# Gate-and-up product of an FFN: P3 of group 1 placed between P6 and P4 of group 0, in the other pair of banks

## The chip, the cores and the metric

The kernel runs on one core of one Trainium2 chip. The metric is the device time of one execution in microseconds, from three runs. The kernel's main engines are TensorE (PE in the rows; PEld is its loading of stationary operands), VectorE (DVE), ScalarE (ACT), GpSimd (POOL) and SyncE (SP), which issues most plain DMAs.

## What is computed

A two-layer encoder trunk on 512 tokens of width 1024. Layer 0 mixes tokens by gated linear attention and RWKV-7, layer 1 by multi-head latent attention; after each mixer stands a SwiGLU FFN with 2816 hidden columns. What the change touches is the first half of that FFN, twice:

```python
def swiglu_ffn(x, w_gate_up, w_down):
    gu = x @ w_gate_up
    gate, up = gu[..., :FFN_HIDDEN], gu[..., FFN_HIDDEN:]
    return (jax.nn.silu(gate) * up) @ w_down

x = layer_norm(DN_ALPHA * x + swiglu_ffn(x, ffn_w_gate_up[i], ffn_w_down[i]), ln_g[i, 1], ln_b[i, 1])
```

## The kernel before

Every large product is done with split operands: a float32 matrix is cast to a high part (`wh`, `xh`) on ScalarE, the remainder is the low part (`wl`, `xl`) by a subtraction on VectorE (`split`, L190 to L193), and a product is high by high, high by low and low by high.

The gate-and-up product (`ffn`, L1139) treats the hidden columns in six groups, 512 columns wide for the first four and 384 for the last two. A group's product of 512 tokens by 1024 by gate and up columns is done with seven products of half size, P1 to P7 (a Strassen-Winograd scheme): each is a sum of parts of x, held in `xh`, `xl`, `Sh` and `Sl`, times a sum of blocks of the weights. P2 is added up in the banks of P1, and P4 in the banks of P7 (`chained`, L1277).

One product (`product`, L1227) has two halves, k2 = 0 and 1. Each half takes a buffer pair for the high and the low part (`parts`, L1214: two `wh`/`wl` pairs, and for every third half, where `spare` is set, the pair called `third`), splits 1024 columns of weights into it and runs 12 matmuls: eight with the high part, then four with the low part. So a product is 24 matmuls.

The weights of a group lie in three float32 buffers, X, Y and Z. X and Z are loaded by SyncE; Y holds in turn the weights of P3, P7, P6 and P4, and X those of P1 and P5. Between them the buffer is changed in place: `more` (L1264) has GpSimd issue two DMAs (512 KB each) that add another block of weights to it. They wait for the two splits that read the old contents, and the next product that reads the buffer waits for them to land.

After its matmuls a product's results are taken from the banks (`step`, L1276 to L1309): copies on ScalarE after P1, P3 and P7; subtractions, additions and multiplications on VectorE after P5 and P6 (eight operations after P6, L1302 to L1305); after P4, for each of the two token tiles, a subtraction on VectorE (L1307), Silu on ScalarE (L1308) and a multiplication on VectorE (L1309). Then `turn(0)` and `turn(1)` (L1311) transpose the finished halves `w` and `v` of the group on TensorE, eight transposes each into two `ps_s` banks, and ScalarE copies them to the hidden tile (L1318). `turn(0)` needs what P6 leaves, `turn(1)` what P4 leaves.

The accumulators (`banks`, L1224) are a pair of the four banks tagged `g`, or the pair `t` and `o`, one bank each. P5 uses t and o, and so does P1, save in group 1.

The order is written out in `work` (L1333): products of neighbouring groups are interleaved. From group 2 on it is P1 of the new group, P4 and turn(0) of the old one, P3, turn(1), P2, the loads of the next group, P7, P5, P6. For group 1, whose P1 and P2 come before the loop, it is P4 of group 0, P3 of group 1, turn(0), turn(1), the loads of group 2, P7, P5, P6. Within an engine the instructions run in a fixed order that the program's builder made from this; it is not always the written one, as the rows below show (a split can stand ahead of copies that are written before it).

Of the kernel before, what the change touches and what calls it, by code (L numbers as in the profile page):

```python
# [1138 lines left out]
def ffn(g, i, hid, ep):  # L1139
# [11 lines left out]
    def E(name):  # L1151
        return ep.tile([P, S], F32, tag="e", name=name, bufs=10)
# [48 lines left out]
    def sums(*names):  # L1201
        for n in names:
            for u in range(2):
                f = whole(u)
                o = {"P3": "P2", "P5": "P1"}.get(n, n)
                if o != n:
                    nc.vector.tensor_tensor(f[o], in0=f["P6"], in1=f[o], op=ALU.subtract)
                out(u, n, f[o])
# [15 lines left out]
    def banks(chain):  # L1224
        return [g.pp.tile([P, S], F32, tag=t, name="ps_g", bufs=4 if t == "g" else 1) for t in ("to" if chain else "gg")]

    def product(name, n, source, acc, first=True, spare=True):  # L1227


        A_ = A[name]  # L1230
        for k2 in range(2):
            h, l = parts(n, spare)
            split(nc, h, l, source(k2))
            for b, w in enumerate((h, l)):
                for q in range(2):
                    k = 2 * k2 + q
                    for u in range(2):
                        for a in range(2 - b):
                            nc.tensor.matmul(acc[u][:, :n], lhsT=A_[a][:, k, P * u:P * u + P], rhs=w[:, q], start=first and k + a + b == 0,  # L1239
                                             stop=k + b == 4, skip_group_check=True)  # L1240

    def group(j):
        c, n = GROUPS[j]
        w = g.I[f"w_gu{i}{j}"]
        W, T, acc, e = {}, {}, {}, [Ctx(), Ctx()]

        def place(k):

            if k == "Z" and j == 1:
                T[k] = [hid.tile(0)[:, 2 * k2:2 * k2 + 2].rearrange("p a b -> p (a b)") for k2 in range(2)]  # L1250
            elif k == "Z":
                T[k] = [g.wp.tile([P, 1024], F32, tag="w", name="w", bufs=2)[:, :2 * n] for k2 in range(2)]
            else:
                t = tp.tile([P, 2048], F32, tag="raw", name="raw", bufs=4)
                T[k] = [t[:, 2 * n * k2:2 * n * k2 + 2 * n] for k2 in range(2)]

        def load(k):
            if k not in T:
                place(k)
            r, q = {"X": (0, 0), "Y": (1, 1), "Z": (1, 0)}[k]  # L1260
            for k2 in range(2):
                nc.sync.dma_start(T[k][k2], w[r, q, k2])

        def more(k, r, q):  # L1264
            for k2 in range(2):
                nc.gpsimd.dma_start(T[k][k2], w[r, q, k2], accum_op=ALU.add)  # L1266

        def row(name, u, i):

            return (hid.row(4 + 2 * i + u) if j == 1 else E(name))[:, :n]  # L1270

        def dve(o, a, op, b):
            nc.vector.tensor_tensor(o, in0=a, in1=b, op=op)
            return o

        def step(name, spare=True):  # L1276
            chained = {"P2": "P1", "P4": "P7"}.get(name)  # L1277
            acc[name] = p = acc[chained] if chained else banks(name == "P5" or name == "P1" and j != 1)
            k = {"P1": "X", "P5": "X", "P2": "Z"}.get(name, "Y")
            product(name, n, lambda k2: T[k][k2].rearrange("p (q n) -> p q n", q=2), p, chained is None, spare)  # L1280
            if name in ("P1", "P3", "P7", "P6"):
                more(k, *{"P1": (0, 1), "P3": (0, 1), "P7": (0, 0), "P6": (1, 0)}[name])
            add, sub = ALU.add, ALU.subtract
            for u in range(2):
                d, y = e[u], p[u][:, :n]
                if name == "P1":
                    d.s1 = row("s1", u, 0)
                    nc.scalar.copy(d.s1, y)
                elif name == "P2":
                    d.g = row("g", u, 1)  # L1290
                    nc.scalar.activation(d.g, y, AF.Silu)
                elif name == "P3":
                    d.w = E("w")[:, :n]
                    nc.scalar.copy(d.w, y)
                elif name == "P7":
                    d.v = E("v")[:, :n]
                    nc.scalar.copy(d.v, y)
                elif name == "P5":
                    dve(d.w, y, add, d.w)
                    dve(d.v, y, add, d.v)  # L1300
                elif name == "P6":
                    d.u = dve(E("u")[:, :n], y, sub, d.s1)  # L1302
                    dve(d.w, d.u, sub, d.w)
                    dve(d.w, d.w, ALU.mult, d.g)
                    dve(d.v, d.u, sub, d.v)  # L1305
                else:
                    dve(d.u, y, sub, d.u)  # L1307
                    nc.scalar.activation(d.u, d.u, AF.Silu)  # L1308
                    dve(d.v, d.v, ALU.mult, d.u)  # L1309

        def turn(half):  # L1311
            for u in range(2):
                y = (e[u].w, e[u].v)[half]
                t = 2 * half + u
                p = g.pp.tile([P, S], F32, tag="s", name="ps_s", bufs=2)[:, :n]
                for m in range(n // P):
                    nc.tensor.transpose(out=p[:, m * P:(m + 1) * P], in_=y[:, m * P:(m + 1) * P], identity=g.C("ident"))  # L1317
                nc.scalar.copy(hid.tile(j)[:, :, t * P:(t + 1) * P], p.rearrange("p (m t) -> p m t", t=P))  # L1318

        return Ctx.of(place=place, load=load, step=step, turn=turn)  # L1320

    gs = [group(j) for j in range(len(GROUPS))]
# [10 lines left out]
    def work():  # L1333

        gs[0].step("P2", False)
        sums("P3")
        gs[0].step("P3", False)
        gs[1].step("P2", False)
        sums("P7", "P5", "P6")
        last = len(gs) - 1  # L1340
        for j, x in enumerate(gs):
            more = j < 4
            if j:
                if j > 1:
                    x.step("P1", more)
                gs[j - 1].step("P4", more)
                if j > 1:
                    gs[j - 1].turn(0)
            if j:
                x.step("P3", more)  # L1350
                for h in range(0 if j == 1 else 1, 2):
                    gs[j - 1].turn(h)
            if j > 1:
                x.step("P2", more)
            if 0 < j < last:
                gs[j + 1].load("Z")
                gs[j + 1].load("X")
                gs[j + 1].load("Y")
            x.step("P7", more and j > 0)
            x.step("P5", more)  # L1360
            x.step("P6", more)
        gs[last].step("P4", False)
        return [lambda h=h: gs[last].turn(h) for h in range(2)]

    return Ctx.of(sink=sink, again=again, load=load, begin=begin, work=work)


# [455 lines left out]
```

## Time and profile before

| | us |
|---|---|
| runs (three) | 1384.99, 1387.27, 1394.15 |
| median | 1387.27 |
| profiled execution, its own time | 1391.69 |
| span of the profile, first to last instruction | 1389.6 |
| TensorE busy | 1342.3 |
| VectorE busy | 921.3 |
| ScalarE busy | 685.1 |
| GpSimd busy | 232.6 |
| mean granted TensorE clock, of full speed | 0.986 |

The profile is of one execution, and its times are microseconds from the start of its span. A timeline row has the start, the duration, the engine, the line, the operation, output and input by the program's names, shapes and a count; in brackets at its end stands how long the engine was idle before it and what ended that. Matmuls overlap: a row's duration is longer than the distance to the next row's start, and it is the distance that counts. The two FFNs stand at about 406 to 585 us and 1025 to 1260 us for their first halves.

### The profile page before, as it was taken

How to read it: one execution, taken by the hardware profiler on the slowest of the kernel's cores; microseconds unless marked ns; L12 is line 12 of the kernel's file. 1: busy time of each engine (PE TensorE's matmuls, PEld its weight loads, DVE VectorE, ACT ScalarE, POOL GpSimd, SP SyncE). 2: the span in 40 equal slices, each digit the busy share in tenths (PEclk: the TensorE clock that was granted, in tenths of full speed). 3: DMA queues.
4: the chain of work that ended last, by engine and by line, in shares of the span. 5: the costliest groups of instructions: out<-in, count | busy, mean ns of one | idle time of the engine just before them, and what ended most of it. 6: DMA issues, size and time to landing. Idle time of an engine off the chain costs nothing.

```text
span 1389.6 us, 21744 instructions
## 1 busy us (share of the span) xinstructions
PE 1342.3 (97%) x8382; PEld 1063.7 (77%) x8382; DVE 921.3 (66%) x1704; ACT 685.1 (49%) x1212; POOL 232.6 (17%) x278
## 2 busy tenths in 40 slices
PE   8899999999999899999999999999999899999997
PEld 6577777766678688998888877666677788997886
DVE  3687677644497666668456367988786766667456
ACT  6653344354536455555334356555445455555341
POOL 2230012122311111126401130000011111120000
PEclk9999999979999999999999999999999999999999
DMA  8563343530468788673325422111277787773232
GB/s 244 111 128 59 70 100 68 113 67 32 157 214 191 163 186 166 149 141 84 103 96 149 118 79 58 55 56 46 92 206 172 161 187 167 145 127 93 91 107 90
DMA packets 74328, 168.15 MB, mean 121 GB/s; under 512 B 21232, under 2 KB 22384, under 8 KB 74096
## 3 DMA queue, kind: packets, MB, share of 16 engines
q0 software_dynamic: 21888, 60.83, 26.2%
q1 hardware_dynamic: 51808, 103.83, 22.9%
q10 hardware_dynamic: 528, 2.10, 0.4%
q8 instruction: 66, 1.08, 0.3%
q14 instruction: 38, 0.31, 0.1%
HBM read 163.77 MB, written 2.95 MB: 120 GB/s over the span
## 4 chain that ended last, share of the span: by engine, by line
PE 62%; issue 14%; DMA 10%; DVE 7%; ACT 3%; POOL 2%; SPq 1%; POOLq 0%; DVEq 0%; ACTq 0%
PE ps_g L1239 12%; PE ps_g L186 10%; PE ps_g L187 10%; PE ps_g L185 10%; DMA raw<-in_w_gu 6%; PE ps_s L1624 3%; PE ps_o L1653 2%; PE ps_c L715 2%; PE ps_t L1640 1%; POOL raw L1266 1%; PE ps_c L674 1%; DMA wl<-in_w_even 1%; PE ps_l L891 1%; PE ps_s L1317 1%; PE ps_c L187 1%
## 5 line engine op out<-in xcount | busy, mean ns | idle before, releaser
L192 DVE TENSOR_TENSOR wl<-raw,wh 128x1024 fp32r<-128x1024 f32 (+1 forms) x120 | 132.7, 1114 | 80.2 <-ACT wh L191 79.8
L191 ACT CAST wh<-raw 128x1024 fp32r<-128x1024 f32 (+1 forms) x120 | 116.0, 968 | 138.2 <-PE ps_g L1239 101.1
L1266 POOL DMA_DIRECT2D raw<-in_w_gu x96 | 83.1, 866 | 494.3 <-DVE wl L192 388.5
L1239 PE MATMUL ps_g<-wh,xh 128*128 128x512 f32 (+1 forms) x320 | 118.9, 372 | 2.0 <-ACT wh L191 2.0
L1239 PE MATMUL ps_g<-wh,xl 128*128 128x512 f32 (+1 forms) x320 | 117.8, 368 | 0.0
L187 PE MATMUL ps_g<-xh,wl 128*128 128x512 f32 (+2 forms) x296 | 113.7, 385 | 3.0 <-DMA wl<-in_w_even 1.8
L185 PE MATMUL ps_g<-xh,wh 128*128 128x512 f32 (+2 forms) x296 | 115.6, 391 | 0.0
L186 PE MATMUL ps_g<-xl,wh 128*128 128x512 f32 (+2 forms) x296 | 114.1, 385 | 0.0
L186 PE MATMUL ps_g<-wl,ah 128*128 128x512 f32 x288 | 112.0, 390 | 0.6 <-DVE wl L192 0.6
L185 PE MATMUL ps_g<-wh,ah 128*128 128x512 f32 x288 | 111.7, 392 | 0.6 <-ACT ah L191 0.4
L187 PE MATMUL ps_g<-wh,al 128*128 128x512 f32 x288 | 110.8, 389 | 0.0
L192 DVE TENSOR_TENSOR wl<-w,wh 128x1024 fp32r<-128x1024 f32 (+2 forms) x79 | 89.4, 1131 | 32.0 <-ACT wh L191 31.6
L191 ACT CAST wh<-w 128x1024 fp32r<-128x1024 f32 (+2 forms) x79 | 76.2, 965 | 60.2 <-PE ps_g L186 36.6
L191 ACT CAST ah<-hid 128x512 fp32r<-128x512 f32 x72 | 43.5, 618 | 98.9 <-PE ps_g L186 98.9
L1239 PE MATMUL ps_g<-wh,Sh 128*128 128x512 f32 (+1 forms) x240 | 90.1, 376 | 0.0
L192 DVE TENSOR_TENSOR al<-hid,ah 128x512 fp32r<-128x512 f32 x72 | 49.2, 695 | 60.9 <-ACT ah L191 60.8
L1239 PE MATMUL ps_g<-wh,Sl 128*128 128x512 f32 (+1 forms) x240 | 89.3, 373 | 0.0
L1239 PE MATMUL ps_g<-wl,xh 128*128 128x512 f32 (+1 forms) x320 | 79.7, 371 | 0.9 <-DVE wl L192 0.9
L215 POOL DMA_DIRECT2D wl<-in_w_even x48 | 41.5, 865 | 229.9 <-ACT wl L214 194.8
L216 ACT CAST wh<-w 128x512 fp32r<-128x512 f32 x64 | 39.3, 617 | 81.5 <-PE ps_g L186 49.7
L1239 PEld LDWEIGHTS ps_g<-wh,xh 128*128 128x128 f32 x320 | 60.1, 188 | 10.5 <-ACT wh L191 2.9
L187 PEld LDWEIGHTS ps_g<-xh,wl 128*128 128x128 f32 (+1 forms) x296 | 56.2, 190 | 14.7 <-DMA wl<-in_w_even 3.0
(461 smaller groups left out, 3269.4 us busy)
## 6 DMA issues: line engine op xcount, KB each, us to landing
raw<-in_w_gu POOLq DMA_DIRECT2D x64, 512.0 KB, 5.7
w<-in_w_dn SPq DMA_DIRECT2D x44, 512.0 KB
raw<-in_w_gu SPq DMA_DIRECT2D x32, 512.0 KB
w<-in_w_even SPq DMA_DIRECT2D x48, 256.0 KB
wl<-in_w_even POOLq DMA_DIRECT2D x48, 256.0 KB, 4.7
raw<-in_w_gu POOLq DMA_DIRECT2D x32, 384.0 KB, 4.8
w<-in_w_gu SPq DMA_DIRECT2D x12, 512.0 KB
raw<-in_w_gu SPq DMA_DIRECT2D x16, 384.0 KB
```

The costliest lines, as they stand in the source:

```text
L185: nc.tensor.matmul(out, lhsT=wh, rhs=xh, start=first, stop=False)
L186: nc.tensor.matmul(out, lhsT=wh, rhs=xl, start=False, stop=False)
L187: nc.tensor.matmul(out, lhsT=wl, rhs=xh, start=False, stop=last)
L191: c = nc.scalar.copy(h, src)
L192: (eng or nc.vector).tensor_tensor(l, in0=src, in1=h, op=ALU.subtract)
L215: nc.gpsimd.dma_start(l, src, accum_op=ALU.add)
L216: nc.scalar.copy(h, w)
L715: nc.tensor.matmul(q[:, CH:] if m else q[:, :CH], lhsT=l, rhs=r, start=m < 2, stop=m != 1)
L1239: nc.tensor.matmul(acc[u][:, :n], lhsT=A_[a][:, k, P * u:P * u + P], rhs=w[:, q], start=first and k + a + b == 0, stop=k + b == 4, skip_gr ...
L1266: nc.gpsimd.dma_start(T[k][k2], w[r, q, k2], accum_op=ALU.add)
L1624: nc.tensor.matmul(p[:, :nk], lhsT=Q[:, h % 4, qb * P:(qb + 1) * P], rhs=K[:, h % 4, :nk], start=True, stop=True)
L1653: nc.tensor.matmul(o[64 * e:64 * e + 64, kb * P:], lhsT=Vv[:, kb, (h - 1 + e) * 64:(h + e) * 64], rhs=t[e][kb][:, kb * P:], start=kb == 0, ...
```

## The change

It alters only the order and the banks around group 1. P3 of group 1 now comes before P4 of group 0 instead of after it; it takes the banks t and o instead of a pair of g; and the two turns of group 0 follow P4 directly, where P3 of group 1 stood between P4 and turn(0). All other groups keep their order.

```diff
         def step(name, spare=True):
             chained = {"P2": "P1", "P4": "P7"}.get(name)
-            acc[name] = p = acc[chained] if chained else banks(name == "P5" or name == "P1" and j != 1)
+            acc[name] = p = acc[chained] if chained else banks(name == "P5" or name == ("P3" if j == 1 else "P1"))
...
         for j, x in enumerate(gs):
             more = j < 4
             if j:
-                if j > 1:
-                    x.step("P1", more)
+
+                x.step("P1" if j > 1 else "P3", more)
                 gs[j - 1].step("P4", more)
-                if j > 1:
-                    gs[j - 1].turn(0)
+                gs[j - 1].turn(0)
+            if j > 1:
+                x.step("P3", more)
             if j:
-                x.step("P3", more)
-                for h in range(0 if j == 1 else 1, 2):
-                    gs[j - 1].turn(h)
+                gs[j - 1].turn(1)
             if j > 1:
                 x.step("P2", more)
```

## Rows read from the trace of the kernel before

**Rows 1.** The page's first part: TensorE's busy time, share of the span, instructions.

```profile
PE 1342.3 (97%) x8382; PEld 1063.7 (77%) x8382; DVE 921.3 (66%) x1704; ACT 685.1 (49%) x1212; POOL 232.6 (17%) x278
```

**Rows 2.** TensorE's waits, whole span: instruction, releaser, us in total, times, longest.

```profile
PE ps_g L1239 <- DVE wl L192: 5.6, 3, 2.4
PE ps_g L1239 <- ACT third L191: 2.6, 4, 0.9
...
PE ps_s L1317 <- ACT hid L1318: 1.0, 2, 0.5
```

**Rows 3.** Timeline of TensorE in the first FFN, P4 of group 0 onward.

```profile
452.99 0.39 PE L1239 MATMUL ps_g<-wh,xh 128*128 128x512 f32 x1
...
456.64 0.50 PE L1239 MATMUL ps_g<-third,xh 128*128 128x512 f32 x1 [0.77 <-ACT third L191]
...
463.83 1.85 PE L1239 MATMUL ps_g<-wl,Sh 128*128 128x512 f32 x4 [2.33 <-DVE wl L192]
...
469.18 1.03 PE L1317 MATMUL ps_s<-cst,w 128*128 128x128 f32 x8
470.72 0.50 PE L1239 MATMUL ps_g<-third,xh 128*128 128x512 f32 x1 [0.51 <-ACT third L191]
...
472.18 1.14 PE L1317 MATMUL ps_s<-cst,v 128*128 128x128 f32 x8 [0.48 <-ACT hid L1318]
...
477.95 0.39 PE L1239 MATMUL ps_g<-wh,Sh 128*128 128x512 f32 x1
...
483.39 0.39 PE L1239 MATMUL ps_g<-wh,Sh 128*128 128x512 f32 x1
```

**Rows 4.** Windows: PE, PEld, DVE, ACT, POOL busy; PEclk; DMA share; GB/s.

```profile
463.80:467.60 3.80, 3.77 (x10) 2.98 (x11) 3.52 (x5) 1.23 (x2) 1.73 (x2) 0.55 0.51 71
```

**Rows 5.** Timeline of TensorE in the second FFN: starts of P4(0) and P5(1).

```profile
1073.52 0.39 PE L1239 MATMUL ps_g<-wh,xh 128*128 128x512 f32 x1
...
1098.60 0.39 PE L1239 MATMUL ps_g<-wh,Sh 128*128 128x512 f32 x1
```

**Rows 6.** Timeline of TensorE one group later: turn 0, turn 1, start of P7.

```profile
499.71 1.03 PE L1317 MATMUL ps_s<-cst,w 128*128 128x128 f32 x8
...
506.06 1.03 PE L1317 MATMUL ps_s<-cst,v 128*128 128x128 f32 x8
...
512.39 0.39 PE L1239 MATMUL ps_g<-wh,xh 128*128 128x512 f32 x1
```

**Rows 7.** Timeline of ScalarE in the first FFN.

```profile
455.54 1.05 ACT L191 CAST third<-raw 128x1024 fp32r<-128x1024 f32 x1 [3.95 <-DMA raw<-in_w_gu]
...
469.62 1.04 ACT L191 CAST third<-raw 128x1024 fp32r<-128x1024 f32 x1 [3.98 <-DMA raw<-in_w_gu]
470.58 1.07 ACT L1294 COPY w<-ps_g 128x512 f32<-128x512 f32 x2
471.53 1.09 ACT L1318 COPY hid<-ps_s 128x512 f32<-128x512 f32 x2
```

**Rows 8.** Timeline of VectorE in the first FFN.

```profile
449.33 0.68 DVE L1273 TENSOR_TENSOR v<-ps_g,v 128x512 f32<-128x512 f32 x1
...
457.76 1.28 DVE L1273 TENSOR_TENSOR u<-ps_g,s 128x512 f32<-128x512 f32 x2
...
462.57 1.21 DVE L192 TENSOR_TENSOR wl<-raw,wh 128x1024 fp32r<-128x1024 f32 x1
463.70 1.28 DVE L1273 TENSOR_TENSOR u<-ps_g,u 128x512 f32<-128x512 f32 x2
...
502.02 1.28 DVE L1273 TENSOR_TENSOR v<-v,u 128x512 f32<-128x512 f32 x2
```

**Rows 9.** Timeline of GpSimd in the first FFN: one DMA issue.

```profile
447.50 0.86 POOL L1266 DMA_DIRECT2D raw<-in_w_gu  x1 [2.00 <-DVE wl L192]
```

**Rows 10.** The tile `raw`: its accumulating DMA issues (ns min/median/max), and landing.

```profile
L1266 POOL DMA_DIRECT2D raw<-in_w_gu x96: 853/862/977, 409.9 to 1251.1; - x96
...
DMA to landing us min/median/max: 4.6/5.5/13.4
```

## The prediction

> **What bounds the kernel now.** I read the page's first part, then the waits of TensorE over the whole span, then its timeline around group 0's last product, and at the same moments the timelines of ScalarE, VectorE and GpSimd. The page has TensorE busy for 97% of the span [rows 1]: only its idle time and its slow stretches can be won back. Most of what it waits for is small and scattered; the reader is to see that the gate-and-up line L1239 waits 5.6 us in 3 places for VectorE's low halves and 2.6 us in 4 places for ScalarE's `third` [rows 2].
>
> I write P4(0) for product P4 of group 0, and P4(0)a, P4(0)b for its halves (k2 = 0 and 1). In the first FFN P4(0) starts at 452.99 and P5(1) at 477.95 [rows 3]. Between lie P4(0), P3(1), the two turns of group 0 and P7(1): 24.96 us. What this work takes undisturbed: one product is 483.39 - 477.95 = 5.44 us [rows 3], and one group later a turn and a product together take 506.06 - 499.71 = 6.35 and 512.39 - 506.06 = 6.33 us [rows 6], so a turn costs 0.9. The sum is 5.44 + 6.35 + 6.33 = 18.12, and 24.96 - 18.12 = 6.84 us are lost here. The second FFN repeats it: 1073.52 to 1098.60 is 25.08 us [rows 5], 6.96 lost. Together 13.80 us, the most the change can give.
>
> Where the 6.84 go [rows 3]: P4(0)b should start at 452.99 + 2.72 = 455.71 and starts at 456.64 (0.93). P3(1)a starts at once, but its four low-half matmuls come at 463.83 after 2.33 us idle. After that wait the granted clock of 463.8 to 467.6 is 0.55 [rows 4], so mostly 1.2 GHz: the 16 matmuls from 463.83 to 469.18 took 5.35 us and would have taken 16 x 5.44/24 = 3.63, a loss of 1.72. P7(1)a waits 0.51 and turn 1 waits 0.48; with the first matmuls after each wait, which run slower, they make up the rest.
>
> The causes. P4(0) reads the weights to which P6(0)'s accumulating load adds. The load of the second half was issued at 447.50 [rows 9], ScalarE's cast waited for it until 455.54 [rows 7]: 8.0 us, longer than one product. VectorE, in order behind that cast, came to P6(0)'s eight combining operations only at 457.76, though P6(0) had ended at 452.99, and to P3(1)a's low half at 462.57 [rows 8]. So one late load costs three times: its own wait, the 2.33 us, and the slow clock.
>
> **What the change does to this.** Instructions: none is added or removed; 24 matmuls, two splits, two copies and two DMA issues of P3(1) move ahead of P4(0) in both FFNs. Their own cost is the same at either place: zero.
>
> Step 1, P3(1) behind P6(0). Its weights (Y of group 1) were loaded at the start. P5(0) ends one product before 452.99, at 447.55, and frees a `wh` buffer, so P3(1)a's cast can run then; its low half follows P5(0)'s operations on VectorE, which end at 450.0 [rows 8], and is done at 451.2, wanted at 452.99 + 1.81 = 454.8. P3(1)b has `third`, free when P6(0)a is done at 450.3; low half done by 452.6, wanted at 457.5. Both stand ahead of P6(0)'s operations, so the 2.33 and the 1.72 go. Banks: t and o were last read by P5(0)'s operations, over at 450.0; in the written pair g P3(1) would have had to wait for P6(0)'s.
>
> Step 2, P4(0) behind P3(1). It starts at 458.43. Its loads have landed (455.5 at the latest), its buffers come free at 452.99 and 455.71, so the cast and low half of each half (2.3 us) are over well before 458.43 and 461.15. P6(0)'s eight operations (4.8 us, 457.76 to 462.57 now [rows 8]) run from 453 to 458; P4(0)a's low half behind them ends at 459.2, wanted at 460.2. The 0.93 goes; of the cover 1.0 us is left.
>
> Step 3, the queues. GpSimd issues in the same order as now (P6(0)'s loads, then P3(1)'s), P3(1)'s at about 451.5 and 452.9. With 5.5 us, the median, they land at 457 and 458.4, with 8.0 at 459.5 and 460.9; P7(1)a's cast must begin by 463.7. SP's next loads into group 0's Y buffer (X of group 3) go out some 5 us later; they are wanted three groups on. Nothing queued behind them is due.
>
> Step 4, what is late next: turn 1. It needs P4(0)'s result through subtract, Silu and multiply, which P3(1) covered until now. One group later P4(1) ends at 499.71 and the two multiplies at 502.02 + 1.28 = 503.30 [rows 6, 8]: 3.6 us. The trace of before shows no turn 1 directly behind its P4, so I bound it. Nothing, if turn 1 stands far enough inside P7(1) (turn 0 and P7(1)a give 0.9 + 2.7 us of cover), and 2.3 us idle plus the slow clock if it stands right behind turn 0 (rival B). I take 0.5 us: in the trace turn 1 already stands three matmuls into P7(1)a and waits 0.48 there [rows 3], and P7(1)a's cast at 469.62 stands ahead of the copies at 470.58 and 471.53 that are written before it [rows 7], so the order follows what is ready.
>
> Behind a waiting turn 1 stands the rest of P7(1), and after it P5(1); no other engine is due for them. P7(1)'s own banks are no wait: P3(1) now ran its first matmuls before 461.5 [rows 3], while P4(0)'s pair was read from 463.70 [rows 8], so the next product takes the pair that is free, and P6(0)'s will be free from about 454.
>
> Sum: 6.84 + 6.96 - 2 x 0.5 = 12.8 us. The profiled execution took 1391.69 us (span 1389.6 and 2.1 around it), so it would take 1378.9. It is 4.4 above the median of the runs, 1387.27; the loss sits in two fixed places, so I take the same 12.8 off the median: **1374.5 us**, 0.92% less.
>
> **The rivals.**
> A is the forecast.
>
> B: turn 1 stands directly behind turn 0 in TensorE's stream. Its input is ready at 463.87 + 3.6 = 467.5 and its last transposes end near 467.9, against 465.6 with everything ready: 2.3 us, as long as the idle stretch after which the clock fell, so 1.7 more. 4.0 a FFN: 13.8 - 8.0 = 5.8 us won, 1381.5. For it: turn 1 is written there, and the transposes at 472.18 were placed before their turn buffer was free. Against: they were placed inside P7(1)a, not in front.
>
> C: the loads collide. From issue to landing the range is 4.6 to 13.4 us [rows 10]. At 13.4 P4(0)b's data land at 460.9 (0.85 late) and P7(1)a's at 464.9 (1.2 late): 2.05 a FFN, 13.8 - 1.0 - 4.1 = 8.7 won, 1378.6. For it: P3(1)'s loads now follow P6(0)'s within 6 us, beside SP's loads. Against: 13.4 is the worst of 96. All 96 issues took between 853 and 977 ns [rows 10], with VectorE busy for two thirds of the span, so none was held up by it. The Trainium skill (SBUF — State Buffer, "SBUF: two separate sides") warns of the opposite: while VectorE runs an operation that takes both of its ports, GpSimd can't write the descriptors of its DMAs. [...]
>
> D, slower: the streams keep the written order. Then P3(1)a's low half stands behind P6(0)'s operations (over at 458.0, low half at 459.2 instead of 454.8: 4.4, and 1.7 of slow clock), and P7(1)a's cast behind turn 1's copies (467.9, a copy of 0.6 and a cast of 1.05: 469.7 instead of 465.7: 4.0, and 1.7). 11.8 us a FFN; it decides from 6.84 upward: 2 x 11.8 - 13.8 = 9.8 slower, 1397.1. For it: P3(1)a's low half does stand behind those eight operations now. Against: it stood there because its buffer came free only with P6(0)'s end, and it stands ahead of P4(0)'s subtract at 463.70, written before it [rows 8].
>
> **How the numbers follow.** A 0.72, B 0.12, C 0.09, D 0.07. The likeliest gives 1374.5. Range: at the low end the full 13.8 (1373.5) less 3 for runs that scatter from 1384.99 to 1394.15; at the high end B and 2 more. 1370.5 to 1383.5 leaves out D and little else. About 1%, 13.9 us, is what a measurement of this kernel can tell from no change. The ceiling lies just there, so A falls above it only by scatter or by a stretch won elsewhere: half of A, 0.35, for faster by over 1%. The other half of A, B, C and most of D are within 1%: 0.62. Slower by over 1% needs D and more: 0.03.
>
> **What would show it.** In the changed profile the stretch from P6(0)'s end to P5(1)'s start should last 18.6 us (18.12 + 0.5) instead of 25 with no wait over 1 us and a clock of 1.00; ScalarE's waits for the landing of `third` should be gone there, VectorE's eight operations should begin at P6(0)'s end, and turn 1 should stand inside P7(1). I am wrong if a wait of over 2 us stands before turn 1 (B), a DMA wait before P7(1) (C), or VectorE's low half of P3(1) behind P6(0)'s operations (D), or if time is lost again in the groups after.

## The result and the profile after

Three runs of the changed kernel took 1371.34, 1374.41 and 1377.04 us, median 1374.41 us. Against the kernel before (median 1387.27 us) the ratio is 0.9889 with an interval of 0.9852 to 0.9927: 12.86 us less between the medians. The forecast was 1374.5 us.

The page's first part answers to [rows 1]. The instruction counts are the same on every engine, and the page has TensorE busy for 12.9 us less.

```profile
PE 1329.4 (97%) x8382; PEld 1057.1 (77%) x8382; DVE 921.4 (67%) x1704; ACT 686.2 (50%) x1212; POOL 231.3 (17%) x278
```

The matmuls are the same; where most of their busy time fell is shown at the end of this section. TensorE's waits over the whole span answer to [rows 2]:

```profile
PE ps_g L1239 <- DVE wl L192: 0.9, 1, 0.9
```

The 5.6 us for VectorE's `wl` are down to 0.9 us, and the rows for ScalarE's `third` and `hid` are gone. What is left stands outside the two stretches that the change touches.

TensorE's timeline answers to [rows 3], and its last two rows to [rows 5] in the second FFN. The rows begin with P3(1), which now stands where P4(0) stood.

```profile
443.94 0.39 PE L1239 MATMUL ps_g<-wh,Sh 128*128 128x512 f32 x1
...
449.38 0.39 PE L1239 MATMUL ps_g<-wh,xh 128*128 128x512 f32 x1
...
452.10 0.39 PE L1239 MATMUL ps_g<-wh,xh 128*128 128x512 f32 x1
...
454.83 1.03 PE L1317 MATMUL ps_s<-cst,w 128*128 128x128 f32 x8
455.62 0.48 PE L1239 MATMUL ps_g<-third,xh 128*128 128x512 f32 x1
...
457.99 1.21 PE L1317 MATMUL ps_s<-cst,v 128*128 128x128 f32 x8
...
462.22 0.39 PE L1239 MATMUL ps_g<-wh,Sh 128*128 128x512 f32 x1
...
1059.88 0.39 PE L1239 MATMUL ps_g<-wh,Sh 128*128 128x512 f32 x1
...
1078.19 0.39 PE L1239 MATMUL ps_g<-wh,Sh 128*128 128x512 f32 x1
```

P6(0) ends at 443.94 and P5(1) starts at 462.22. No row in between has a wait: P3(1) takes 5.44 us, P4(0)a 2.72 and P4(0)b 2.73, which is what a product and half a product take undisturbed (5.44 and 5.44 / 2). Turn 1 stands ten matmuls into P7(1)a. The same two stretches as windows (duration; PE, PEld, DVE, ACT, POOL busy; granted clock; DMA share; GB/s):

```profile
443.94:462.22 18.28, 18.28 (x89) 15.13 (x88) 14.37 (x18) 10.35 (x15) 2.20 (x3) 1.00 0.91 199
1059.88:1078.19 18.31, 18.31 (x90) 15.15 (x88) 14.35 (x18) 10.34 (x15) 2.17 (x3) 1.00 0.88 187
```

The stretch took 24.96 and 25.08 us before [rows 3, 5]. The gain is 6.68 and 6.77, together **13.45 us**, with TensorE busy throughout and the clock at 1.00.

ScalarE's timeline (to be held against [rows 7]), VectorE's ([rows 8]) and GpSimd's ([rows 9]), in this order:

```profile
448.23 1.06 ACT L191 CAST wh<-raw 128x1024 fp32r<-128x1024 f32 x1 [3.94 <-DVE v L1273]
450.07 1.05 ACT L191 CAST third<-raw 128x1024 fp32r<-128x1024 f32 x1 [0.78 <-DMA raw<-in_w_gu]
...
452.56 1.05 ACT L191 CAST wh<-raw 128x1024 fp32r<-128x1024 f32 x1 [0.47 <-DMA raw<-in_w_gu]
```

```profile
440.88 1.21 DVE L192 TENSOR_TENSOR wl<-raw,wh 128x1024 fp32r<-128x1024 f32 x1
442.01 1.22 DVE L192 TENSOR_TENSOR third<-raw,third 128x1024 fp32r<-128x1024 f32 x1
443.92 1.29 DVE L1273 TENSOR_TENSOR u<-ps_g,s 128x512 f32<-128x512 f32 x2 [0.69 <-PE ps_g L1239]
...
448.73 2.35 DVE L192 TENSOR_TENSOR wl<-raw,wh 128x1024 fp32r<-128x1024 f32 x2
...
457.13 1.29 DVE L1273 TENSOR_TENSOR v<-v,u 128x512 f32<-128x512 f32 x2
```

```profile
438.58 0.86 POOL L1266 DMA_DIRECT2D raw<-in_w_gu  x1 [2.00 <-DVE wl L192]
442.38 0.86 POOL L1266 DMA_DIRECT2D raw<-in_w_gu  x1 [2.94 <-DVE wl L192]
443.52 0.86 POOL L1266 DMA_DIRECT2D raw<-in_w_gu  x1 [0.27 <-DVE third L192]
```

The low halves of P3(1) (440.88 and 442.01) are done before P6(0) ends, and P6(0)'s operations begin at 443.92, at its end, instead of 4.8 us after it. The two casts of P7(1) still wait for a DMA, but at 450.07 and 452.56, long before their matmuls at 455.62 and 459.50. A DMA wait in ScalarE's rows is no loss as long as it ends in time.

The two profiled executions differ by more than the change: 1391.69 and 1371.34 us, spans 1389.6 and 1369.2, so 20.4 us. Of these 13.45 lie in the two stretches. Another 9.05 lie ahead of the first: P6(0) ends at 452.99 there and at 443.94 here, although up to that point TensorE, VectorE and ScalarE run the same sequence of operations in both kernels, save for two neighbouring matmuls (at 159.8 and 157.6 us) that changed places and for the last splits, which are P3(1)'s instead of P4(0)'s. About 2.1 us go the other way between the two FFNs, and behind the second stretch the two are alike. The windows from the start to P6(0)'s end, first of the kernel before and then of the changed one:

```profile
0.00:452.99 452.99, 431.65 (x4012) 321.81 (x4013) 287.19 (x598) 227.73 (x421) 93.59 (x114) 0.97 0.50 120
```

```profile
0.00:443.94 443.94, 422.20 (x4012) 315.99 (x4013) 287.81 (x600) 229.41 (x423) 96.24 (x116) 1.00 0.51 122
```

The same 4012 matmuls were busy for 9.45 us more at a granted clock of 0.97 than at 1.00: in matmuls that both kernels share, one execution had the slower clock. That is most of what the page's first part shows as less busy time, and it has nothing to do with the change. It is why the stretches, not the spans, are compared below.

### The profile page after: what moved, and what is told of

The parts are those of the page before. It is cut to its first block, busy times and chain, and to the rows that moved or that the text cites. A ratio compares the mean times of both kernels' runs of the same rounds, so it can differ in the third digit from the quotient of the medians.

```text
span 1369.2 us, 21744 instructions
## 1 busy us (share of the span) xinstructions
PE 1329.4 (97%) x8382; PEld 1057.1 (77%) x8382; DVE 921.4 (67%) x1704; ACT 686.2 (50%) x1212; POOL 231.3 (17%) x278
## 4 chain that ended last, share of the span: by engine, by line
PE 63%; issue 13%; DMA 10%; DVE 7%; ACT 3%; POOL 2%; SPq 1%; POOLq 0%; DVEq 0%; ACTq 0%
PE ps_g L1239 12%; PE ps_g L186 11%; PE ps_g L187 10%; PE ps_g L185 10%; DMA raw<-in_w_gu 6%; PE ps_s L1623 3%; PE ps_o L1652 2%; POOL raw L1266 2%; PE ps_c L715 2%; PE ps_t L1639 2%; PE ps_c L674 1%; DMA wl<-in_w_even 1%; SPq L637 1%; PE ps_c L187 1%; PE ps_l L891 1%
## 5 line engine op out<-in xcount | busy, mean ns | idle before, releaser
L1239 PE MATMUL ps_g<-wh,xh 128*128 128x512 f32 (+1 forms) x328 | 122.1, 373 | 2.2 <-ACT wh L191 2.2
L1239 PE MATMUL ps_g<-wh,xl 128*128 128x512 f32 (+1 forms) x328 | 120.9, 369 | 0.0
L185 PE MATMUL ps_g<-xh,wh 128*128 128x512 f32 (+2 forms) x296 | 114.1, 386 | 0.0
L185 PE MATMUL ps_g<-wh,ah 128*128 128x512 f32 x288 | 111.6, 392 | 0.7 <-ACT ah L191 0.6
L1239 PE MATMUL ps_g<-wh,Sh 128*128 128x512 f32 (+1 forms) x232 | 85.4, 369 | 0.0
L1239 PE MATMUL ps_g<-wh,Sl 128*128 128x512 f32 (+1 forms) x232 | 85.0, 367 | 0.0
L1239 PEld LDWEIGHTS ps_g<-wh,xl 128*128 128x128 f32 x328 | 61.6, 188 | 7.6
```

Of the source, the lines that this page charges most:

```text
L185: nc.tensor.matmul(out, lhsT=wh, rhs=xh, start=first, stop=False)
```

## The experiments

Theories: **L**, one late load behind P6(0) costs several times over, and P3(1) covers it; **K**, the time came from the clock elsewhere; **V**, VectorE's order alone makes the loss; **B**, the pair of banks alone makes the gain. "The stretch" is always from P6(0)'s end to P5(1)'s start, first and second FFN.

### The changed kernel again

No edit.

> The changed kernel once more, against the kernel before in the same rounds. Theory L (the late accumulating load behind P6(0) cost 6.7 us in each FFN, and P3(1) now covers it): 13.4 us faster, ratio 0.990, and the stretch P3(1) to P7(1) lasts 18.3 us in both FFNs. Rival K (most of the difference came from a higher granted clock in other stages, by chance): the ratio comes out nearer to 1, 0.995 or above, with the same 18.3 us.

Measured over six runs: median 1374.64 us (1369.21 to 1379.43), against 1384.04 us for 17 runs of the kernel before on the same chip, ratio 0.9913, interval 0.9879 to 0.9947. The stretch took 18.28 and 18.30 us. These medians differ by 9.40 us, 4 us less than the two stretches give; 13.45 us are 0.97% of 1387, inside both intervals. The stretch repeats to 0.03 us while whole runs scatter by 10 us: it is the better measure. Since it alone accounts for the difference, K is not needed; the ratio by itself, with an interval that ends just below K's 0.995, would hardly have excluded it.

### The change in the first FFN only

```diff
-            acc[name] = p = acc[chained] if chained else banks(name == "P5" or name == "P1" and j != 1)
+            acc[name] = p = acc[chained] if chained else banks(name == "P5" or name == ("P3" if j == 1 and i == 0 else "P1") and (j != 1 or i == 0))
...
+                late = j == 1 and i == 1
+                if not late:
+                    x.step("P1" if j > 1 else "P3", more)
                 gs[j - 1].step("P4", more)
-                if j > 1:
+                if not late:
                     gs[j - 1].turn(0)
-            if j:
+            if j > 1 or j and late:
                 x.step("P3", more)
-                for h in range(0 if j == 1 else 1, 2):
-                    gs[j - 1].turn(h)
+            if j:
+                if late:
+                    gs[j - 1].turn(0)
+                gs[j - 1].turn(1)
```

> The change in the first FFN alone, the second as before. L: half the gain, 6.7 us, ratio 0.995; the stretch between P6(0) and P5(1) lasts 18.3 us in the first FFN and 25.1 in the second. K: no relation between the two stretches and the total; anything from 0.99 to 1.00.

Measured over twelve runs: median 1379.03 us (1374.29 to 1387.90), ratio 0.9967, interval 0.9938 to 0.9995. The stretch took 18.28 us in the first FFN and 26.30 in the second. Half the change gives a gain in its own FFN and none in the other. The second FFN missed the expected 25.1 by 1.2 us. Its waits in TensorE's timeline, and a window behind them:

```profile
1067.61 1.20 PE L1239 MATMUL ps_g<-wl,Sh 128*128 128x512 f32 x4 [2.37 <-DVE wl L192]
...
1074.24 0.50 PE L1239 MATMUL ps_g<-third,xh 128*128 128x512 f32 x1 [1.82 <-ACT third L191]
...
1075.70 1.54 PE L1317 MATMUL ps_s<-cst,v 128*128 128x128 f32 x8 [0.50 <-ACT hid L1318]
```

```profile
1075.70:1080.35 4.65, 4.65 (x17) 3.87 (x18) 2.45 (x2) 4.24 (x6) 1.72 (x2) 0.63 0.70 120
```

These are the three last waits of [rows 3], but the one ahead of P7(1) is 1.82 us instead of 0.51. P3(1)'s own load decides there, and it was no slower: from issue to landing it took 5.18 us, and 5.45 in the kernel before. TensorE came sooner. Behind the wait of 2.37 us the clock stayed at 1.00 here, and the 16 matmuls up to turn 0 took 3.77 us instead of 5.35. The slow clock came only behind the wait of 1.82 us (0.63 in the window), where no later wait took it up: from P7(1)a's start to P5(1)'s it took 8.87 us, and 7.23 before. In the old order the loss is therefore not a constant.

### The old order without the late load

```diff
             product(name, n, lambda k2: T[k][k2].rearrange("p (q n) -> p q n", q=2), p, chained is None, spare)
-            if name in ("P1", "P3", "P7", "P6"):
+            if name in ("P1", "P3", "P7", "P6") and (name != "P6" or j):
                 more(k, *{"P1": (0, 1), "P3": (0, 1), "P7": (0, 0), "P6": (1, 0)}[name])
```

> The order and banks of before, but without the two accumulating loads behind P6(0), so P4(0) uses P6(0)'s weights: this leaves out part of the computation. VectorE's order is that of before. L: without a late load the three losses go together (0.93, 2.49 and 1.72 us): the stretch P4(0) to P7(1) falls from 24.96 to about 19.8 us, and TensorE's clock stays at 1.00. Rival V (P3(1)'s low half costs its wait because it stands behind P6(0)'s eight operations, load or no load): the 2.3 us wait and the slow clock stay, about 24 us.

Measured in one run: 1373.19 us, and a stretch of 19.98 and 19.93 us. VectorE kept the old order: P3(1)a's low half stands behind P6(0)'s operations, as its timeline shows.

```profile
443.98 1.29 DVE L1273 TENSOR_TENSOR u<-ps_g,s 128x512 f32<-128x512 f32 x2 [0.69 <-PE ps_g L1239]
...
448.80 1.21 DVE L192 TENSOR_TENSOR wl<-raw,wh 128x1024 fp32r<-128x1024 f32 x1
```

Without the load the eight operations begin at P6(0)'s end and the low half comes in time. The wait of 2.33 us and the slow clock are both gone, with the order unchanged. V falls. What stays are two waits further on in TensorE's timeline, and a clock of 1.00 in the window over the stretch:

```profile
456.76 0.50 PE L1239 MATMUL ps_g<-third,xh 128*128 128x512 f32 x1 [0.83 <-ACT third L191]
...
458.22 1.14 PE L1317 MATMUL ps_s<-cst,v 128*128 128x128 f32 x8 [0.49 <-ACT hid L1318]
```

```profile
444.00:464.00 20.00, 18.68 (x90) 15.11 (x89) 14.36 (x18) 10.00 (x15) 3.45 (x4) 1.00 0.66 140
```

So the late load behind P6(0) accounts for 24.96 - 19.98 = 4.98 us in the first FFN. The way by which it does is seen in GpSimd's timeline, in the first issue behind P3(1), of the kernel before and then of this one:

```profile
464.07 0.86 POOL L1266 DMA_DIRECT2D raw<-in_w_gu  x1 [15.71 <-DVE wl L192]
```

```profile
450.31 0.86 POOL L1266 DMA_DIRECT2D raw<-in_w_gu  x1 [19.86 <-DVE wl L192]
```

This load waits for P3(1)a's low half, and P7(1)a needs its data. Counted from P6(0)'s end (452.99 and 444.01), the low half began at 9.58 before and at 4.79 here, the load was issued at 11.08 and at 6.30, and P7(1)a began at 17.73 and at 12.75: the whole 4.98 us reach TensorE through the late low half and the load behind it. The other 19.98 - 18.28 = 1.70 us are waits for that load and of turn 1. The change wins those too, because P3(1) issues its loads earlier and turn 1 stands further inside P7(1).

### The old order, with six of P6(0)'s eight operations and P4(0)'s written behind P3(1)

```diff
+        def rest():
+            for d in e:
+                six(d)
+            for u in range(2):
+                four(e[u], acc["P4"][u][:, :n])
...
-                    dve(d.w, d.u, sub, d.w)
-                    dve(d.w, d.w, ALU.mult, d.g)
-                    dve(d.v, d.u, sub, d.v)
-                else:
-                    dve(d.u, y, sub, d.u)
-                    nc.scalar.activation(d.u, d.u, AF.Silu)
-                    dve(d.v, d.v, ALU.mult, d.u)
+                    if j:
+                        six(d)
+                elif j:
+                    four(d, y)
...
                 x.step("P3", more)
+                if j == 1:
+                    gs[0].rest()
```

Here `six` is the three lines it replaces for each token tile, and `four` the subtraction, Silu and multiplication after P4.

> The order and banks of before, but six of P6(0)'s eight VectorE operations, and those of P4(0), are written behind P3(1), so that P3(1)'s low half stands ahead of them. L with its chain (late load, then VectorE's run, then the clock): the wait of 0.8 us before P4(0)b stays, the 2.3 us wait and the 1.7 us of slow clock go: 20.7 us for the stretch. If the 2.3 us were the load itself and not VectorE's queue: 24 to 25 us as before.

Measured in one run: 1386.29 us, a stretch of 26.91 and 26.67 us. This is the clear miss of the study: the expected 20.7 was 6 us too low. The step it was to test did hold: in neither FFN does TensorE wait for `wl`, and from P4(0)'s start to turn 0 it took 455.81 - 444.43 = 11.38 us, where the kernel before took 469.18 - 452.99 = 16.19 [rows 3]. The first FFN tests little, because P4(0)b waited only 0.20 us there and not the expected 0.8. In the second FFN P4(0)b waited 0.96 us, about as before (0.91), and still no second wait followed. So the 2.3 us are VectorE's queue behind the late cast, and not the load directly. But another queue took its place. TensorE's timeline, ScalarE's, and a window:

```profile
463.64 1.97 PE L1332 MATMUL ps_s<-cst,v 128*128 128x128 f32 x8 [4.18 <-ACT hid L1333]
```

```profile
457.16 1.04 ACT L191 CAST third<-raw 128x1024 fp32r<-128x1024 f32 x1 [7.80 <-DMA raw<-in_w_gu]
458.11 0.63 ACT L1285 ACTIVATE u<-u 128x512 f32<-128x512 f32 x1
...
462.99 1.08 ACT L1333 COPY hid<-ps_s 128x512 f32<-128x512 f32 x2
```

```profile
463.60:468.59 4.99, 4.95 (x17) 4.27 (x17) 0.59 (x1) 2.69 (x4) 0.86 (x1) 0.53 0.88 162
```

ScalarE waits 7.80 us for P7(1)a's load, and P4(0)'s Silu and the copies of turn 0 stand behind that cast in its order, though they are written before it. Turn 1 needs its `ps_s` banks emptied by those copies, waits 4.18 us for them, and after that the clock is 0.53. This is rival D's kind of loss: a short operation behind a long DMA wait in an engine's fixed order.

### The banks alone, and the order alone

The old order with P3(1) in t and o (against the kernel before), and the new order with P3(1) in a pair of g (against the changed kernel):

```diff
-            acc[name] = p = acc[chained] if chained else banks(name == "P5" or name == "P1" and j != 1)
+            acc[name] = p = acc[chained] if chained else banks(name == "P5" or name == ("P3" if j == 1 else "P1"))
```

```diff
-            acc[name] = p = acc[chained] if chained else banks(name == "P5" or name == ("P3" if j == 1 else "P1"))
+            acc[name] = p = acc[chained] if chained else banks(name == "P5" or name == "P1" and j != 1)
```

> P3(1) in the banks t and o, in the order of before. L: the bank was never what P3(1) waited for, so the stretch P4(0) to P7(1) stays at 25 us with the same waits of 0.8 and 2.3 us. Rival B (the other pair of banks is what sets P3(1) free): the 2.3 us wait goes, 21 us or less.

> The order of the change, with P3(1) in a pair of g. Every pair of g is then taken by P7(0)/P4(0) or by P6(0) when P3(1) begins, so it waits for VectorE's two subtractions behind P6(0): about 1 us of wait (0.3 to the first one's start, 0.7 for it), nothing else: 18.3 + 1 = 19.3 us for the stretch. B: most of the gain is lost, 23 us or more.

The banks alone: 1391.57 us in one run, stretch 24.60 and 24.92 us, with the same late low half. B falls. TensorE's timeline in the first FFN, and the stretch as a window:

```profile
465.26 1.21 PE L1239 MATMUL ps_g<-wl,Sh 128*128 128x512 f32 x4 [2.37 <-DVE wl L192]
...
471.90 0.50 PE L1239 MATMUL ps_g<-third,xh 128*128 128x512 f32 x1 [1.79 <-ACT third L191]
```

```profile
454.52:479.12 24.60, 19.29 (x89) 14.95 (x88) 15.52 (x19) 10.99 (x15) 3.48 (x4) 1.00 0.59 127
```

This stretch also shows what the slow clock costs in the old order. Here the clock stayed at 1.00 throughout, behind the wait of 2.37 us too, and yet the stretch is only 0.36 us shorter than the 24.96 of the kernel before: the wait for P3(1)'s load is 1.79 us instead of 0.51 and takes up what the faster matmuls gave.

The order alone: 1376.30 us in one run, stretch 18.81 and 18.84 us, half a microsecond longer than with the banks of the change. In TensorE's timeline two matmuls of P4(0)a stand ahead of P3(1)'s, where the wait for the banks was expected; it seems that the builder filled that wait with them.

```profile
449.11 0.50 PE L1239 MATMUL ps_g<-wh,xh 128*128 128x512 f32 x1 [0.23 <-ACT wh L191]
449.45 0.39 PE L1239 MATMUL ps_g<-wh,xl 128*128 128x512 f32 x1
449.68 0.40 PE L1239 MATMUL ps_g<-wh,Sh 128*128 128x512 f32 x1
```

So of the 6.7 us a FFN the order alone gives 6.2, and the banks add 0.5.

### The new order, with P6(0)'s loads issued twice

```diff
             if name in ("P1", "P3", "P7", "P6"):
-                more(k, *{"P1": (0, 1), "P3": (0, 1), "P7": (0, 0), "P6": (1, 0)}[name])
+                for t in range(2 if name == "P6" and j == 0 else 1):
+                    more(k, *{"P1": (0, 1), "P3": (0, 1), "P7": (0, 0), "P6": (1, 0)}[name])
```

> The changed kernel with the two accumulating loads behind P6(0) issued twice, one after the other, so that the weights of P4(0) are not those that the reference needs. It asks how much cover P3(1) leaves. L: the second half's data landed at 448.2 in the changed profile and were wanted at 451.0, so 2.8 us are left; a second pass takes 5.5 to 8 us more, 3 to 5 us too late: a wait of that size before P4(0)b, slow clock after it, stretch 22 to 25 us. If P4(0) had no need to wait for them: 18.3 us.

Measured in one run: 1395.77 us, stretch 26.24 and 27.14 us. TensorE's timeline and a window:

```profile
465.07 0.79 PE L1239 MATMUL ps_g<-wh,xh 128*128 128x512 f32 x1 [3.84 <-ACT wh L191]
```

```profile
465.00:469.00 4.00, 3.93 (x9) 3.14 (x10) 2.20 (x2) 2.04 (x4) 0.00 (x0) 0.50 1.04 222
```

P4(0)b waited 3.84 and, in the second FFN, 4.88 us, inside the expected 3 to 5. The clock fell behind the wait (0.50 here), as expected. The stretch was longer than the expected 22 to 25, because turn 1 waited as well (0.80 and 1.76 us), which the expectation had not counted. One product of cover suffices for one load and not for two: the cover is finite, as L says.

### Carried on: the last group

The changed kernel still waits in group 5, which has no next group to lie beside. Here its P3 stands ahead of P4 of group 4 as well, and its products are in another order.

```diff
+            if j == last:
+                x.step("P3", more)
+                gs[j - 1].step("P4", more)
+                gs[j - 1].turn(0)
+                x.step("P1", more)
+                gs[j - 1].turn(1)
+                for name in ("P7", "P2", "P6", "P5"):
+                    x.step(name, more)
+                continue
```

Besides, P3 and P6 of that group take t and o, and six of its P6's eight operations come after P5's.

> The changed kernel with the same idea in the last group, whose P4 also follows its P6 directly: order P3, P4 of group 4, P1, P7, P2, P6, P5, P4, so that each added-to load has a product between; P3 and P6 in t and o; P6's last six operations behind P5's. L: of the waits of TensorE at the end of each FFN's first half (0.77 before P4, 1.05 before a turn, 0.32 and 0.39 behind it) most of the first three go: about 1.5 us a FFN, 3 us in all, ratio to the kernel before 0.988. Rival: the tail of VectorE work behind P5 comes later by as much as is won: 0.990 to 0.991, no wait less in sum.

Measured over six runs: median 1368.29 us (1366.43 to 1377.59), against 1384.19 us for eleven runs of the kernel before on that chip, ratio 0.9898, interval 0.9857 to 0.9939. TensorE's timeline from turn 1 of group 4 to the first matmul of the down product (L185), first of the changed kernel and then of this one:

```profile
598.46 0.81 PE L1317 MATMUL ps_s<-cst,v 128*128 128x128 f32 x6
...
616.69 0.44 PE L1239 MATMUL ps_g<-wh,xh 128*128 128x384 f32 x1 [0.77 <-ACT wh L191]
...
620.11 0.52 PE L1317 MATMUL ps_s<-cst,w 128*128 128x128 f32 x3 [1.05 <-DVE w L1273]
...
624.04 0.50 PE L185 MATMUL ps_g<-wh,ah 128*128 128x512 f32 x1 [0.39 <-ACT ah L191]
```

```profile
598.26 0.81 PE L1323 MATMUL ps_s<-cst,v 128*128 128x128 f32 x6
...
620.49 0.52 PE L1323 MATMUL ps_s<-cst,w 128*128 128x128 f32 x3 [0.97 <-DVE w L1273]
...
622.10 0.73 PE L185 MATMUL ps_g<-wh,ah 128*128 128x512 f32 x2
```

In these two profiles that stretch fell from 25.58 to 23.84 us, and in the second FFN from 25.06 to 23.84. The wait of 0.77 us for ScalarE is gone, the one of a microsecond before the last turn stays. But the 2.96 us that this makes are too much. The changed kernel's other profile has 25.02 and 25.04 us for the stretch, so 25.58 is not its usual length. And the down product then takes a little longer: from its first matmul to its last it took 100.03 and 99.91 us here, and 99.66 to 99.70 in the four of the changed kernel. From turn 1 of group 4 to the last matmul of the down product the changed kernel took 125.26 and 124.76 us in one profile and 124.68 and 124.71 in the other, and this one 123.87 and 123.75. About 1 us a FFN is won, 1.8 to 2.4 us together, and not the expected 3; the rival's "no wait less in sum" did not come out either. The intervals of the two ratios overlap too much to show either. (The first half of the first FFN lasts longer than the 585 us given at the top: its last gate-and-up matmul starts at 638.72 us in the kernel before.)

## Why the prediction was right

**The ceiling.** The prediction put the stretch at 18.12 us undisturbed and the loss at 6.84 + 6.96 = 13.80 us. The stretches after are 18.28 and 18.31, so 13.45 of the 13.80 were won, against a forecast of 12.8.

**One late load costs three times.** Two parts of this held: the late load makes the loss, and VectorE's queue carries it on. The third, the slow clock as a cost of its own, did not. The old order without that load gave back 4.98 us in the first FFN; what it left, 1.70, is the fourth term, the waits of P7(1) and turn 1. The terms 0.93 + 2.33 + 1.72 make 4.98 too, but with the 2.49 us by which the low half came late they make 5.14, so the equality is chance. Deferring VectorE's operations separated the second term from the first. The 1.72 us of slow clock were mostly hidden: in the kernel before TensorE still had to wait for P3(1)'s load behind the slow matmuls (0.51 us), and with the clock at 1.00 that wait was 1.79 us and the stretch 24.60. The total was right all the same, because the change removes everything on this way at once.

Nor do the runs show that a wait of this length must slow the clock. Behind the waits of 2.33 to 2.38 us for `wl` in five stretches of the old order, the 16 matmuls took 5.35, 5.37 and 5.37 us in three and 3.81 and 3.77 in two. Behind four waits of 3.84 to 4.88 us the clock fell each time (0.53 after 4.18, 0.50 after 3.84), and the stretches of the new order and of the old one without the late load, with no wait over 0.83 us, kept 1.00. What decides between the cases is not shown.

**Step 1** held. Both low halves of P3(1) ran ahead of P6(0)'s operations (440.88 and 442.01 against 443.92). The banks, costed as a wait avoided, are worth 0.5 us a FFN and not more: in the written pair two matmuls of P4(0)a stood where the wait was expected.

**Step 2** held. Left over was to be 1.0 us before P4(0)a's low half. The two low halves that begin at 448.73 take 2.35 us together, so the first is done at about 449.9, wanted at 451.20: 1.3 us. P4(0)b's cast ended at 449.29, wanted at 452.10, which leaves 2.8 us. Its row names VectorE as what it waited for (the operation before it ended at 448.21), but its load, issued at 438.58, landed after 9.5 us at 448.1, so the two lie too close to say which one set it.

**Step 3** held, with other sizes. The prediction let the loads land after 5.5 or 8.0 us. P7(1)'s casts waited for theirs until 450.07 and 452.56, that is 7.7 and 9.0 us after the issues at 442.38 and 443.52, and P6(0)'s second took 9.5. One sign that the prediction named did not come: ScalarE still waits for the landing of `third` here (0.78 us before 450.07). It costs nothing, because it ends in time. Rival C was right that these loads take longer than the median; but its price needs 13.4, and P7(1)'s casts still began 5.6 and 6.9 us ahead of their matmuls. The issues and the landing times, from the view of the tile `raw` between 430 and 470 us:

```profile
L1266 POOL DMA_DIRECT2D raw<-in_w_gu x9: 865/865/883, 430.1 to 466.8; - x9
...
DMA to landing us min/median/max: 5.4/5.6/9.5
```

No issue took over 883 ns, with VectorE busy for 14.37 of the 18.28 us. The hold that the Trainium skill warns of (SBUF — State Buffer, "SBUF: two separate sides") is for VectorE's operations in a two-port mode, with a float32 copy as the example. All 18 VectorE operations of this window are TENSOR_TENSOR, so the window does not test it. What makes one of these loads take 5.4 us and another 9.5 stays open.

**Step 4** is the term that was mis-sized. Turn 1 was to cost 0.5 us a FFN; all that exceeds 18.12 is 0.16 and 0.19. The chain after P4(0) was as long as predicted: P4(0) ended at 454.83 and the multiplications at 457.13 + 1.29 = 458.42, 3.6 us. But the builder put ten matmuls of P7(1)a between the turns, not three, and turn 1 started at 457.99 without a wait. That is the 0.65 us by which the gain beat 12.8.

**B and D** fell: no wait of over 2 us stands before turn 1, and nothing of P3(1) stands behind P6(0)'s operations. D's mechanism exists, as the deferred operations showed, only not in this order.

Taking the gain off the median of the runs, rather than off the slow profiled execution, was right: the 6.95 us by which the two profiles differ beyond the stretches are scatter. The predicted total came within 0.1 us, which is luck: the runs scatter by 6 to 14 us, and six more had a median gain of 9.40. The stretch is the real test, 18.6 predicted and 18.28 measured.

## What to carry to other kernels

When an in-place load is needed by the next product and takes longer than that product's predecessor, move a product that needs no load between them, and count everything queued behind the waiting cast: here the wait itself was 0.93 of 4.98 us. An operation that is moved back in one engine's order can put another engine's work behind a DMA wait, so ask where such waits will stand before moving it. A slow clock ahead of a later DMA wait can cost little (here 0.36 of 1.72 us), because the later wait takes it up: add up losses along the chain that ends last, not side by side. Compare a stretch between two named instructions when whole runs scatter by as much as the gain.

## What the runs showed of the hardware that was not expected

- The granted clock differed between two executions in the same matmuls, 0.97 and 1.00 over the first 4012, and that was worth 9 us, more than the change in one FFN. It can fall where TensorE has no wait: in the kernel before it was 0.50 from 280 to 290 us, with TensorE busy for all 10 us, while the changed kernel had 1.00 from 250 to 300 us.

```profile
280.00:290.00 10.00, 10.00 (x50) 5.27 (x46) 1.16 (x3) 3.14 (x5) 4.71 (x6) 0.50 0.42 66
```

- The 512 KB accumulating loads vary more than their median says: 5.6 us in the median between 430 and 470 us of the changed profile and up to 9.5. The wait of P7(1)a does not follow them: it was 0.51, 1.82 and 1.79 us where its load took 5.45, 5.18 and 5.19, with a slow clock ahead of it in the first case only.
